# Row sums of a 64 MB array: the first load of SyncE in three transfers by partitions, and the first whole group on SyncE's queue

## Chip, core and metric

The kernel runs on one core of a Trainium2 chip. The metric is the device time of one execution in microseconds (us); lower is better. The core's engines follow their own instruction streams and meet at semaphores: VectorE (DVE in the profile), ScalarE (ACT), GpSimd (POOL), SyncE (SP) and TensorE (PE, without work here). Transfers between memory and the on-chip SBUF run on 16 DMA engines. SP, ACT and POOL each issue transfers on a queue of their own (q1, q10 and q0 in the profile), and all three queues use the same 16 engines. SBUF has 128 partitions.

## What is computed

The input x has 32 x 512 x 1024 float32 values. Each of the 16,384 rows of 1024 values is summed:

```python
def reference(x: np.ndarray) -> np.ndarray:
    return np.sum(x, axis=-1).astype(np.float32)
```

That is 67.11 MB read once, and 65 KB written.

## The kernel before

Each of the 128 partitions takes J = 128 rows. They lie in two regions: region a holds 16 rows of each partition (2,048 rows of x), region b the other 112. Within a region a partition's rows follow each other in memory, so that one partition's share of a transfer is one contiguous run. `rows_from(j, n)` names rows j to j + n of every partition.

There are three buffers `bufs` of 16 rows for each partition (64 KB). The work goes in this order:

- the entry load: 8 rows of each partition (FIRST = 8, the first half of the last group, `tail` = 112), 4.19 MB, into buffer 0, issued by SP at line 97 through `load(..., "first")`;
- groups 0 to 6, each 16 rows of each partition, 8.39 MB, into buffers 1, 2, 0, 1, 2, 0, 1, issued by POOL at line 99;
- the last 8 rows of each partition, as four transfers of lines 175 to 181, into buffer 2 and the tile `ends`, issued by POOL at line 99 too.

`issue_first_load_at_entry` (lines 9 to 27) works on the finished program. It takes the first DMA instruction of SP that it finds behind the entry block, and puts it into the entry block ahead of SP's drain, that is, ahead of the barrier at which all engines meet before the kernel's body begins. It moves one instruction and returns.

DVE takes the entry load and groups 0 to 5 in that order (lines 171 to 173): it waits for the load's semaphore, sums all rows with one `tensor_reduce` (line 106), and adds one to the semaphore `summed`. Group 6 and the last 8 rows form the tail. DVE sums rows of it with `halves` (line 115) and ACT with `act` (line 135), each row by itself, as the transfers land.

A group's load may start when its buffer is free. POOL issues groups 0 and 1 at once, since their buffers are empty, and waits for `summed` to reach g - 1 before group g from group 2 on (lines 152 and 153). Group 2 so waits for the entry load's sum, group 3 for that of group 0, and so on. The four last transfers wait for `summed` to reach 6 (line 174), the sum of group 4.

ACT stores the sums of groups 0 to 6 and of the entry load near the end, as two transfers (lines 210 and 211). The last store is SP's (line 227), and SP's wait for it is the last instruction.

Of the kernel before, what the change touches and what calls it, by code (L numbers as in the profile page):

```python
# [30 lines left out]
def kernel(  # L31
# [5 lines left out]
    nc = tc.nc  # L37
# [12 lines left out]
    BIG = 16  # L50
# [15 lines left out]
    def rows_from(j, n):  # L66
        if j < ONE:
            return x_a[:, j : j + n, :]
        return x_b[:, j - ONE : j - ONE + n, :]

    last = J // BIG - 1
    tail = last * BIG
    FIRST = 8
# [14 lines left out]
    def semaphore(name):  # L88
        return ctx.enter_context(nc.semaphore(name=name))

    def block_of(t, a, n):
        return t[:, a * dim : (a + n) * dim].rearrange("p (n d) -> p n d", d=dim)

    def load(dst, src, k):
        sem = semaphore(f"load_{k}")
        if k == "first":
            nc.sync.dma_start(out=dst, in_=src).then_inc(sem, 16)
        else:
            nc.gpsimd.dma_start(out=dst, in_=src, single_packet=True).then_inc(sem, 16)  # L99
        return sem  # L100

    summed = semaphore("summed")

    def vec(j, block):
        n = block.shape[1]
        return nc.vector.tensor_reduce(  # L106
            out=sums[:, j : j + n],
            in_=block,
            axis=mybir.AxisListType.X,
            op=mybir.AluOpType.add,  # L110
        )
# [31 lines left out]

    t = bufs[0]
    block = block_of(t, 0, FIRST)
    landed = load(block, rows_from(tail, FIRST), "first")
    loads = [(landed, tail, block)]
    for g in range(last):  # L150
        t = bufs[(1 + g) % 3]
        if g > 1:
            nc.gpsimd.wait_ge(summed, g - 1)
        block = block_of(t, 0, BIG)
        loads.append((load(block, rows_from(g * BIG, BIG), g), g * BIG, block))

# [3 lines left out]
    t = bufs[(1 + last) % 3]  # L162
# [5 lines left out]
    whole6, whole8 = ends[:, :six], ends[:, six:]  # L168
    right6, right8 = whole6[:, 1:-1], whole8[:, 1:-1]
    nc.vector.memset(ends[:, six - 1 :: whole8.shape[-1]], 0.0)  # L170
    for landed, first, block in loads[:-1]:
        nc.vector.wait_ge(landed, 16)
        vec(first, block).then_inc(summed, 1)
    nc.gpsimd.wait_ge(summed, last - 1)
    line = rows_from(j, 8).rearrange("p n d -> p (n d)")
# [1 line left out]
            (right6, 5 * dim + SIXTH), (right8, 7 * dim + EIGHTH))  # L177
    five, seventh, sixth, eighth = (
        load(dst, line[:, at : at + dst.shape[-1]], f"run_{k}")
        for k, (dst, at) in enumerate(runs)  # L180
    )
# [3 lines left out]

    paired = semaphore("paired")
    carried = semaphore("carried")
    landed, first, block = loads[-1]
    n_pairs = 10
    nc.vector.wait_ge(landed, 16)  # L190
    for q in range(n_pairs):
# [67 lines left out]
```

## Time and profile before

| what | us |
|---|---|
| median of 3 runs | 160.6 (160.52 to 160.64) |
| the profiled execution | 160.88 |
| span of the profiled execution | 159.6 |
| DVE busy | 121.6 (76% of the span) |
| ACT busy | 11.0 (7%) |
| POOL busy | 6.2 (4%) |
| DVE's idle time before sums of line 106, all ended by a load | 32.2, of which 22.9 before the first sum |
| POOL's idle time at line 99 ended by sums of DVE | 120.9 |
| issue to landing, SP's entry load | 24.5 |
| issue to landing, the seven groups, median | 40.5 |

Reading from HBM was 67.11 MB, on average 421 GB/s over the span. The span starts with SP's issue of the entry load. A DMA's issue is a short instruction on the engine that issues it; what the transfer takes is the time to its landing. A packet here is one partition's contiguous run: 32 KB in the entry load, 64 KB in a group. The records of the trace give each packet its start, duration, queue and size, but not its engine.

### The profile page before, as it was taken

How to read it: one execution, taken by the hardware profiler on the slowest of the kernel's cores; microseconds unless marked ns; L12 is line 12 of the kernel's file. 1: busy time of each engine (PE TensorE's matmuls, PEld its weight loads, DVE VectorE, ACT ScalarE, POOL GpSimd, SP SyncE). 2: the span in 40 equal slices, each digit the busy share in tenths (PEclk: the TensorE clock that was granted, in tenths of full speed). 3: DMA queues.
4: the chain of work that ended last, by engine and by line, in shares of the span. 5: the costliest groups of instructions: out<-in, count | busy, mean ns of one | idle time of the engine just before them, and what ended most of it. 6: DMA issues, size and time to landing. Idle time of an engine off the chain costs nothing.

```text
span 159.6 us, 123 instructions
## 1 busy us (share of the span) xinstructions
DVE 121.6 (76%) x42; ACT 11.0 (7%) x19; POOL 6.2 (4%) x15
## 2 busy tenths in 40 slices
DVE  0000008999998999949999499986999679995986
ACT  3000000000000000000000000000000000000995
POOL 3000000010001000010000100010000220000000
DMA  7999996996997979969969969969969979898993
GB/s 263 526 394 394 435 600 279 526 509 279 526 444 345 526 345 444 526 279 509 526 263 526 526 263 526 509 279 526 509 279 526 460 329 526 378 411 364 438 402 127
DMA packets 2000, 67.18 MB, mean 421 GB/s; under 512 B 624, under 2 KB 624, under 8 KB 848
## 3 DMA queue, kind: packets, MB, share of 16 engines
q0 software_dynamic: 1424, 62.92, 91.2%
q1 hardware_dynamic: 288, 4.20, 6.6%
q10 hardware_dynamic: 288, 0.06, 0.2%
HBM read 67.11 MB, written 0.07 MB: 421 GB/s over the span
## 4 chain that ended last, share of the span: by engine, by line
DMA 74%; DVE 22%; POOL 1%; issue 1%; POOLq 0%
DMA rows<-in_x_dram 56%; DVE sums L106 22%; DMA ends<-in_x_dram 19%; POOL rows L99 1%; DVE ends L115 0%; DVE sums L115 0%; POOLq L43 0%
## 5 line engine op out<-in xcount | busy, mean ns | idle before, releaser
L106 DVE TENSOR_REDUCE sums<-rows 128x16 f32<-128x16384 f32 (+1 forms) x7 | 111.9, 15999 | 32.2 <-DMA rows<-in_x_dram 32.2
L135 ACT ACTIVATE unread<-rows 128x1024 f32<-128x1024 f32 x9 | 9.1, 1013 | 145.5 <-DMA rows<-in_x_dram 145.5
L115 DVE CUSTOM_DVE_ANT_0 rows<-rows 128x512 f32<-128x512 f32 (+2 forms) x15 | 9.0, 659 | 2.6 <-DMA rows<-in_x_dram 2.6
L99 POOL DMA_DIRECT2D rows<-in_x_dram x9 | 4.9, 546 | 122.4 <-DVE sums L106 120.9
L135 ACT ACTIVATION_READ_ACCUMULATOR unread<-rows 128x1 f32 x9 | 1.7, 186 | 0.0
L135 ACT ACT_TABLE_LOAD x1 | 1.3, 1283 | 1.4 <-PEq L43 1.4
L170 DVE MEMSET ends<- 128x2 f32 x1 | 0.1, 60 | 1.5 <-PEq L43 1.5
L115 DVE DVE_READ_ACCUMULATOR2_ANT sums<- 128x1 f32 x15 | 1.2, 80 | 0.0
L99 POOL DMA_DIRECT2D ends<-in_x_dram x2 | 1.1, 543 | 0.0
L115 DVE CUSTOM_DVE_ANT_0 ends<-ends 128x271 f32<-128x271 f32 (+1 forms) x2 | 0.7, 364 | 0.1
L115 DVE DVE_READ_ACCUMULATOR2_ANT ends<- 128x1 f32 x2 | 0.2, 84 | 0.0
L243 POOL MEMSET const-float32-0.0<- 128x1 f32 x1 | 0.1, 99 | 0.2 <-issue 0.2
L243 POOL MEMSET const-bfloat16-1.0<- 128x1 bf16 x1 | 0.1, 103 | 0.0
L243 POOL MEMSET const-float32-1.0<- 128x1 f32 x1 | 0.1, 99 | 0.0
L243 POOL MEMSET const-uint8-127<- 128x1 uint8 x1 | 0.1, 99 | 0.0
## 6 DMA issues: line engine op xcount, KB each, us to landing
rows<-in_x_dram SPq DMA_DIRECT2D x1, 4096.0 KB, 24.5
rows<-in_x_dram POOLq DMA_DIRECT2D x1, 2802.0 KB, 27.9
rows<-in_x_dram POOLq DMA_DIRECT2D x1, 899.0 KB, 29.6
ends<-in_x_dram POOLq DMA_DIRECT2D x1, 270.0 KB, 29.7
ends<-in_x_dram POOLq DMA_DIRECT2D x1, 125.0 KB, 29.5
rows<-in_x_dram POOLq DMA_DIRECT2D x7, 40.5
out_dram<-sums ACTq DMA_DIRECT2D x1, 48.0 KB, 1.6
out_dram<-sums ACTq DMA_DIRECT2D x1, 8.0 KB, 1.5
```

The source lines that it names most:

```text
L99: nc.gpsimd.dma_start(out=dst, in_=src, single_packet=True).then_inc(sem, 16)
L106: return nc.vector.tensor_reduce(out=sums[:, j : j + n], in_=block, axis=mybir.AxisListType.X, op=mybir.AluOpType.add,)
L115: return nc.vector.tensor_tensor_reduce(out=src[:, :n], in0=src[:, :n], in1=src[:, n:], scale=1.0, scalar=0.0, op0=mybir.AluOpType.add, op ...
L135: nc.scalar.activation(out=unread[n_acts % len(unread)][:, :], in_=src, func=mybir.ActivationFunctionType.Copy, accum_out=sums[:, j : j + ...
L170: nc.vector.memset(ends[:, six - 1 :: whole8.shape[-1]], 0.0)
L243: nc = _bacc.Bacc("TRN2", target_bir_lowering=False, num_devices=1)
```

## The change

The entry load becomes three transfers of SP on one semaphore: partitions 0, 4, 8, ... (32 of them), then 2, 6, 10, ... (32), then the odd ones (64). DVE waits for 48 instead of 16 before the first sum. Group 0 is issued by SP too, behind them. POOL's first load is then group 1, and it waits for `summed` to reach 1; group 2 waits for 1 as before. `issue_first_load_at_entry` isn't changed.

```diff
     def load(dst, src, k):
         sem = semaphore(f"load_{k}")
-        if k == "first":
+        if k == 0:
             nc.sync.dma_start(out=dst, in_=src).then_inc(sem, 16)
         else:
             nc.gpsimd.dma_start(out=dst, in_=src, single_packet=True).then_inc(sem, 16)
...
     t = bufs[0]
-    block = block_of(t, 0, FIRST)
-    landed = load(block, rows_from(tail, FIRST), "first")
-    loads = [(landed, tail, block)]
+    entry = semaphore("entry")
+    block, src = block_of(t, 0, FIRST), rows_from(tail, FIRST)
+    parts = ((0, 4), (2, 4), (1, 2))
+    for at, step in parts:
+        nc.sync.dma_start(out=block[at::step], in_=src[at::step]).then_inc(entry, 16)
+    loads = [(entry, 16 * len(parts), tail, block)]
     for g in range(last):
         t = bufs[(1 + g) % 3]
-        if g > 1:
-            nc.gpsimd.wait_ge(summed, g - 1)
+        if g > 0:
+            nc.gpsimd.wait_ge(summed, max(1, g - 1))
         block = block_of(t, 0, BIG)
-        loads.append((load(block, rows_from(g * BIG, BIG), g), g * BIG, block))
+        loads.append((load(block, rows_from(g * BIG, BIG), g), 16, g * BIG, block))
...
-    for landed, first, block in loads[:-1]:
-        nc.vector.wait_ge(landed, 16)
+    for landed, count, first, block in loads[:-1]:
+        nc.vector.wait_ge(landed, count)
         vec(first, block).then_inc(summed, 1)
...
-    landed, first, block = loads[-1]
+    landed, _, first, block = loads[-1]
```

## The prediction

> **What bounds the kernel now.** I read the chain of waits first, then the DMA part of the page, then the timeline, then the trace's records of single DMA packets. The chain that ended last, by engine and by line:
>
> ```profile
> DMA 74%; DVE 22%; POOL 1%; issue 1%; POOLq 0%
> DMA rows<-in_x_dram 56%; DVE sums L106 22%; DMA ends<-in_x_dram 19%; POOL rows L99 1%; DVE ends L115 0%; DVE sums L115 0%; POOLq L43 0%
> ```
>
> Three quarters of it is DMA. The 22% of DVE are two sums that freed a buffer for a load; they look like a bound and are none, because the load that they released stood behind another one in the same queue. The DMA queues and the time from issue to landing say so (columns: queue, packets, MB, share of 16 engines; then the issues):
>
> ```profile
> q0 software_dynamic: 1424, 62.92, 91.2%
> q1 hardware_dynamic: 288, 4.20, 6.6%
> ...
> rows<-in_x_dram SPq DMA_DIRECT2D x1, 4096.0 KB, 24.5
> ...
> rows<-in_x_dram POOLq DMA_DIRECT2D x7, 40.5
> ```
>
> 91.2% + 6.6% is 98% of what 16 engines can do in the span. A group load takes 40.5 us from issue to landing, though its bytes need half of that, so one whole group is always queued ahead. The timeline gives the pace (start, duration, engine, line, what, idle before it):
>
> ```profile
> 0.00 0.38 SPq L97 DMA_DIRECT2D rows<-in_x_dram  x1
> ...
> 1.44 1.28 ACT L135 ACT_TABLE_LOAD   x1 [1.44 <-PEq L43]
> ...
> 1.94 1.20 POOL L99 DMA_DIRECT2D rows<-in_x_dram  x2 [1.50 <-POOLq L43]
> 24.48 25.81 DVE L106 TENSOR_REDUCE sums<-rows 128x8 f32<-128x8192 f32 x2 [22.91 <-DMA rows<-in_x_dram]
> 33.46 0.53 POOL L99 DMA_DIRECT2D rows<-in_x_dram  x1 [30.31 <-DVE sums L106]
> 50.59 0.53 POOL L99 DMA_DIRECT2D rows<-in_x_dram  x1 [16.60 <-DVE sums L106]
> 51.08 17.22 DVE L106 TENSOR_REDUCE sums<-rows 128x16 f32<-128x16384 f32 x1 [0.79 <-DMA rows<-in_x_dram]
> 68.60 0.53 POOL L99 DMA_DIRECT2D rows<-in_x_dram  x1 [17.48 <-DVE sums L106]
> 70.43 17.22 DVE L106 TENSOR_REDUCE sums<-rows 128x16 f32<-128x16384 f32 x1 [2.13 <-DMA rows<-in_x_dram]
> ```
>
> The sums start at 51.08 and 70.43, 19.35 us apart, and so on to the tail. A group is 128 x 64 KB = 8.389 MB, and 8.389 MB in 19.35 us is 433.5 GB/s. In the packet records each engine moves 64 KB in 2.42 us; 8 of those are 19.36 us, the whole period. The engines never pause between groups. All 67.11 MB at 433.5 GB/s take 154.8 us and the chain's last load lands at 157.42, so only about 2.6 us of the load stream is not streaming. That start, a lower rate, or a DVE that falls behind are the only ways to move the end.
>
> The start in the packet records: the SP load is issued at 0.00, the 16 engines start their first 32 KB packet between 1.02 and 1.54, and end it between 2.89 and 3.21, but for one that ends at 3.52 (later such packets take 1.21). That laggard stays: at each group's landing 15 engines report within about 0.33 us and the last one 0.32 us after them.
>
> **The change part by part.**
>
> *Entry load in three pieces.* In the built program only the quarter of 32 partitions is ahead of the barrier; the second quarter, the half of 64 and group 0 follow behind SP's branch. So the stream starts with an instruction of the same kind at the same place. Its cost with 32 rows is not in the trace. Every SP and ACT issue here has 128 rows: 0.38 and 0.35 us on SP, 0.37 and 0.46 on ACT. From the end of the issue to the first packet it is 0.64 for the load and 0.50 for the stores. The farthest row is POOL's first issue, 0.67 against its later 0.53. I bound the shift of the stream by 0.2 us earlier (half of SP's 0.38 saved) and 0.3 later (0.67 less 0.38), and take 0, the nearest row.
>
> SP's later issues are hidden by the first quarter. ACT begins its first instruction behind the barrier at 1.44, POOL at 1.94. SP at 1.9 at the latest, plus 1.02 to the first packet, makes 2.9, while a quarter is two 32 KB packets per engine, 1.02 + about 1.95 + 1.22 = 4.2. The half is ready one issue later (3.3 to 3.6), group 0 another. Cover of 1.3 us; if it were gone, each us of delay would be a us of time.
>
> Two more transfers make two more seams in each engine's stream. The seams between groups cost 19.35 - 19.36 = 0, with a bound of 0.02 each from rounding. I take 0.
>
> *The laggard.* If its 0.3 us came from the first burst, the other order of descriptors may remove it (-0.3), keep it (0), or make another (+0.3). The first addresses that are read are mostly the same, so I take 0.
>
> *Group 0 on SP, behind the entry load.* Its 8.389 MB now run after the entry load instead of beside it. The entry load lands at about 2.7 + 4.194 MB / 433.5 GB/s = 12.4 instead of 24.48. DVE sums it in 8.69, to 21.1. POOL then issues groups 1 and 2 (before: group 1 at 2.6, group 2 at 33.46; line 152's wait is now ahead of group 1, and all of POOL's later loads are queued behind it). Group 0 still has bytes to move, so the engines don't run dry; the records of before show one 32 KB packet of SP's queue alternating with one 64 KB packet of POOL's. If group 0 goes as 64 KB packets, the queues share evenly from about 22.5: group 0 has 4.0 MB left, 8.0 MB pass, and it lands at 22.5 + 18.5 = 41.0, against about 31 before. POOL coming later makes that earlier (first packet at 26.0: 37.4).
>
> So DVE begins group 0 at 41.0 instead of 33.17, and has six sums of 17.23 us to the pairs, which cannot start before group 6 lands at 147.84. 41.0 + 103.4 = 144.4: 3.4 us to spare, and by group 5 (41.0 + 86.2 = 127.2 against its landing at 128.49) DVE waits for DMA again. The buffers come free later, at 58.2, 75.4, 92.7, 109.9 and 127.1, each more than 10 us before the load ahead lands (70.4, 89.8, 109.1, 128.5, 147.8). From 128.49 on nothing differs.
>
> *Sum:* 0 (issue) + 0 (seams) + 0 (laggard) + 0 (order) = no change. The profiled run took 160.88 us, its span 159.6, and 1.3 lie around it; the median of the runs is 160.6, 0.3 below the profiled one. I forecast 160.6. Bounds of this case: -0.3 and +0.3, 160.3 to 160.9.
>
> **The rivals.**
>
> 1. *The engines get in each other's way in the three pieces: slower.* For it: the full rate (16 x 64 KB in 2.42 us) is only shown for transfers over all 128 partitions; nothing shows how 32 or 64 strided rows are dealt out. If two engines meet on one way into SBUF in each step, the 4.194 MB run at half rate: 9.7 us more, 170.3; if the pairs get out of step and meet half of the time, 4.8 more, 165.4. It decides as soon as the pieces lose more than 0.3 us, 3% of their 9.7. [...] Chance 0.25.
> 2. *The start is cleaner: faster.* A shorter transfer is issued sooner, or the laggard goes: its lead of 0.3 gone is 160.3, all engines ending like the earliest (2.89 for 3.52) 160.0. For it: the end is that laggard's, all the way. Against: the first packet's extra 0.7 us is there with any number of rows. Chance 0.22.
> 3. *The entry issue takes longer with this form.* +0.3 or a little more by POOL's dearer issue, 160.9 to 161.2; the barrier, which waits for SP, then moves too. Chance 0.10.
> 4. *Group 0 gets a third of the engines.* If SP's queue carries its rows as 32 KB packets, as it does now, group 0 lands at 22.5 + 12.0 MB / 433.5 GB/s = 50.2. DVE ends its six sums at 153.6 and the tail's 9.6 us of work at 163.2 instead of 158.10: 165.7. Against: POOL's queue carries 64 KB rows in one packet. Chance 0.05.
>
> **How the numbers follow.** The forecast has 0.38. Less than 0.2% (0.3 us) is about what a measurement here can't tell from no change. Faster is rival 2: 0.22; same the forecast: 0.38; slower rivals 1, 3 and 4: 0.40. The range starts at 160.0 (all engines like the earliest) and ends at 165.8 (rival 4, and rival 1 at half effect). It leaves out the stronger half of rival 1 and a little of rival 2, some 0.17. The forecast's own range is 160.3 to 160.9.
>
> **What would show it.** Right: an SP issue near 0.38, first packets near 1.0 and no pause at the seams; the first sum at about 12.4, the second at 37 to 41; 19.35 us between the sums from group 5 on. The landing of the entry load tests rival 1: 22 us for half rate. The laggard's 0.3 us at the landings tests rival 2, SP's first issue rival 3, and a start of the second sum near 50 rival 4. I am wrong if the pieces run below 433 GB/s, if SP's second issue comes after about 3 us, or if DVE is still summing group 5 when group 6 has landed.

## The result, and the profile after

The changed kernel takes 161.81 us (median; 161.29 to 162.09) against 160.6 before: a ratio of 1.0073, 95% interval [1.0053, 1.0092]. It is slower by 1.2 us, and its runs spread more. The profiled execution took 161.69 us, with a span of 160.4; it lies 0.1 below its median, and the profiled one of before 0.3 above, so the two profiles differ by 0.8 us and not by 1.2.

The timeline of the changed kernel up to the sum of group 5 (start, duration, engine, line, what, idle before it), with the lines that answer to those of before:

```profile
0.00 2.94 SPq L152 DMA_DIRECT2D rows<-in_x_dram  x3
...
1.84 1.28 ACT L135 ACT_TABLE_LOAD   x1 [1.84 <-PEq L43]
...
2.99 0.58 SPq L97 DMA_DIRECT2D rows<-in_x_dram  x1
13.23 8.69 DVE L106 TENSOR_REDUCE sums<-rows 128x8 f32<-128x8192 f32 x1 [11.25 <-DMA rows<-in_x_dram]
22.22 1.20 POOL L99 DMA_DIRECT2D rows<-in_x_dram  x2 [21.79 <-DVE sums L106]
39.81 68.60 DVE L106 TENSOR_REDUCE sums<-rows 128x16 f32<-128x16384 f32 x4 [17.90 <-DMA rows<-in_x_dram]
...
109.96 17.22 DVE L106 TENSOR_REDUCE sums<-rows 128x16 f32<-128x16384 f32 x1 [1.55 <-DMA rows<-in_x_dram]
...
129.31 17.22 DVE L106 TENSOR_REDUCE sums<-rows 128x16 f32<-128x16384 f32 x1 [2.12 <-DMA rows<-in_x_dram]
```

Three things are to be seen. ACT starts behind the barrier 0.40 us later (1.84 for 1.44): SP's first issue ends at 0.54 instead of 0.38, and the way from there to the barrier's end is longer by the rest, 0.24. The entry load is complete at 13.2 (before: 24.5), so only half as long after its issue as before, since nothing is interleaved with it any more. And from 109.96 on DVE waits for each load again. The sum of group 5, at 129.31, starts 0.82 later than before (128.49), and the span is 0.8 longer: the whole loss of this profile is there before the tail begins.

The chain of waits, by engine and by line:

```profile
DMA 64%; DVE 32%; issue 1%; SPq 1%; POOL 1%
DMA rows<-in_x_dram 45%; DVE sums L106 32%; DMA ends<-in_x_dram 19%; SPq L152 1%; POOL rows L99 1%; DVE ends L115 0%; DVE sums L115 0%
```

DVE's share rises from 22% to 32%. That is no new bound: the chain runs through a sum that released a load which then stood in a queue, as before (issued at 74.45 and landed 35.48 us later, while a group's bytes take 19.36). The new entry is SPq L152, the issue of the second and third piece. In order of time (start, duration, what):

```profile
1.83 0.47 SPq L152
2.30 0.05 issue
2.35 0.59 SPq L152
```

The trace's records of DMA packets show where the stream lost its time (start + duration, 32 KB each where nothing stands behind it). They don't name the engine; a row is put together by taking the packet that starts where another one ends. Two of the 16 engines of the changed kernel, and one of before:

```
after   1.33+1.78 3.11+1.23 | 4.34+1.21 5.55+1.68 | 7.23+1.35 8.58+1.21 9.79+1.21 10.99+1.21 | 12.21+2.42(64 KB)
after   1.59+1.89 3.48+1.23 | 4.71+2.10 6.80+1.21 | 8.02+1.21 9.23+1.21 10.44+1.21 11.64+1.21 | 12.86+2.42(64 KB)
before  1.02+2.06 3.08+1.21   4.29+1.22 5.51+1.21   6.72+2.42(64 KB) 9.14+1.21
```

The bars are the seams between the transfers. The first packets start 0.3 us later than before. Both packets of the first quarter take no longer than before (1.78 to 1.89 and 1.23 in these rows, 2.06 and 1.21 in that of before). Behind the first seam packets take up to 2.10 instead of 1.21, on one engine at once and on the other a packet later. By about 11 us it is over, and group 0's 64 KB take the usual 2.42.

### The profile page after: what moved, and what is told of

Its sections match the earlier page's. It is cut to its first block, busy times and chain, and to the rows that moved or that the text cites. A ratio compares the mean times of both kernels' runs of the same rounds, so it can differ in the third digit from the quotient of the medians.

```text
span 160.4 us, 125 instructions
## 1 busy us (share of the span) xinstructions
DVE 121.4 (76%) x42; ACT 11.0 (7%) x19; POOL 5.6 (4%) x14
## 4 chain that ended last, share of the span: by engine, by line
DMA 64%; DVE 32%; issue 1%; SPq 1%; POOL 1%
DMA rows<-in_x_dram 45%; DVE sums L106 32%; DMA ends<-in_x_dram 19%; SPq L152 1%; POOL rows L99 1%; DVE ends L115 0%; DVE sums L115 0%
## 5 line engine op out<-in xcount | busy, mean ns | idle before, releaser
L99 POOL DMA_DIRECT2D rows<-in_x_dram x8 | 4.4, 548 | 123.7 <-DVE sums L106 123.7
```

## The experiments

Each kernel was timed in rounds with the kernel before on the same chip, and its ratio is to that. "Lead" below is the time from the start of the next transfer's issue to the moment at which the median engine reaches the seam, by the packet records.

### Order or pieces

The entry load as one transfer, the rest as changed:

```diff
-    parts = ((0, 4), (2, 4), (1, 2))
+    parts = ((0, 1),)
```

> The entry load is one transfer over 128 partitions again; group 0 stays on SyncE and GpSimd's waits stay. In the changed kernel's packets the first 32 KB of the engines end 0.25 us later than before, and the second and third transfer lose another 0.6 us; from group 0 on nothing is lost. If the whole loss belongs to the three pieces (theory A), this kernel takes 160.6 +- 0.15, with SP's first issue at 0.38 and first packets at 1.02 again. If the order of the queues (group 0 behind the entry load, group 1 waiting) costs something of its own (theory B), it takes 161.0 or more.

160.63 us, ratio 0.9995 [0.9986, 1.0003]. Its first sum starts at 12.11:

```profile
0.00 0.36 SPq L152 DMA_DIRECT2D rows<-in_x_dram  x1
1.42 0.33 SPq L97 DMA_DIRECT2D rows<-in_x_dram  x1
12.11 8.69 DVE L106 TENSOR_REDUCE sums<-rows 128x8 f32<-128x8192 f32 x1 [10.55 <-DMA rows<-in_x_dram]
```

That is 1.12 before the changed kernel's 13.23, nearly all of the 1.2 us. The start of the first sum is thus a good single reading for what the entry costs, as long as nothing is interleaved with the entry load.

The reverse, three pieces with group 0 on POOL and POOL's waits as before:

```diff
-        if k == 0:
+        if k == "none":
...
-        if g > 0:
-            nc.gpsimd.wait_ge(summed, max(1, g - 1))
+        if g > 1:
+            nc.gpsimd.wait_ge(summed, g - 1)
```

> Three pieces as in the changed kernel, but group 0 on GpSimd and its waits as before. Theory A (pieces alone): 161.4 to 162.0, like the changed kernel. Theory B (order): 160.6 to 160.9.

161.84 us, 1.0071 [1.0055, 1.0086], like the changed kernel. The pieces cost all of it; SyncE's group 0 and GpSimd's added wait cost nothing.

### What about the pieces: their place or their shape

All three ahead of the barrier (the helper moves three instructions instead of one):

```diff
-        load = insts.pop(at)
+        early = [insts[k] for k in at[:3]]
...
-        main.instructions = entry[:k] + [load] + entry[k:]
+        main.instructions = entry[:k] + early + entry[k:]
```

> As the changed kernel, but all three pieces are issued ahead of the barrier, one after the other. Theory C (the second and third piece are issued too late behind the barrier, at 1.83 and 2.35, so that the engines start them without having read ahead): with issues at about 0.54 and 1.05 the loss of 0.6 us goes, and 161.1 or less remain, the later first packet alone. Theory D (the strided pieces disturb each other on the engines whenever they are issued): 161.5 to 162.1, and the packets between 4.3 and 9 us still take 1.3 to 2.1 us instead of 1.21.

161.0 us, 1.0022 [1.0013, 1.003].

```profile
0.00 1.81 SPq L150 DMA_DIRECT2D rows<-in_x_dram  x3
...
3.12 0.35 SPq L95 DMA_DIRECT2D rows<-in_x_dram  x1
...
12.40 8.69 DVE L104 TENSOR_REDUCE sums<-rows 128x8 f32<-128x8192 f32 x1 [9.14 <-DMA rows<-in_x_dram]
```

0.8 of the 1.2 us are gone, though the barrier moves to 3.1 and with it group 0's issue. In the packet records every packet behind the first takes 1.21 or 1.22. The first packets still start at 1.33. This is theory C's outcome as to the time of the issue; that the engines read ahead was not shown.

Three pieces that each span all 128 partitions, at the places of the change:

```diff
-    parts = ((0, 4), (2, 4), (1, 2))
+    parts = ((0, 2), (2, 2), (4, 4))
-    for at, step in parts:
-        nc.sync.dma_start(out=block[at::step], in_=src[at::step]).then_inc(entry, 16)
+    for at, n in parts:
+        nc.sync.dma_start(out=block[:, at : at + n], in_=src[:, at : at + n]).then_inc(entry, 16)
```

> Three pieces of the same sizes, issued at the same places, but each spans all 128 partitions: rows 0 to 1, 2 to 3 and 4 to 7 (8, 8 and 16 KB for each partition). Theory D (strided partitions are to blame): 160.5 to 160.8, SP's first issue 0.38. Theory C (late issue behind the barrier): the loss of about 0.6 us at the second transfer stays, 161.1 to 161.5; only the start is that of before.

162.02 us, 1.0079 [1.0067, 1.0092]: theory D, that the stride disturbs the engines, falls. Theory C has the loss, but not its size: 1.4 us without any stride, above the 161.5 that it allowed, while the start is that of before (issue 0.37, first packets at 1.00).

Two theories were then set against each other. Theory C2: what counts is the lead, and one of about 2 us is too short. Theory E: every seam behind the barrier between small transfers costs about 0.7 us, whatever the lead. The same three pieces by rows, all ahead of the barrier:

> Three pieces by rows (2, 2, 4), all ahead of the barrier, issued at about 0, 0.4 and 0.8. Theory C2: both losses gone, 160.5 to 160.8, with SP's first issue 0.37 and no slow packets. Theory E: 161.2 to 162.0.

160.67 us, 1.0001 [0.9992, 1.001]. Both losses are gone, with three transfers and two more seams than with one. A seam cost nothing here where the next transfer had been issued early enough (3.8 us ahead at the first one).

### The stride alone, and contiguous pieces

Even partitions at the entry, odd ones behind the barrier, `parts = ((0, 2), (1, 2))`:

> Two strided pieces, even partitions at the entry, odd ones behind the barrier. The seam is reached near 6.9, a lead of more than 4 us, so theory C2 sees no loss there and leaves the strided first issue alone (0.54 instead of 0.37, first packets 0.3 later): 160.9 to 161.1. If the strided pieces cost more than their issue: 161.3 or more.

161.06 us, 1.0033 [1.0022, 1.0043]. With a seam at 7.0 (lead 5.2) only the late start is left: 0.44 us.

Contiguous pieces:

```diff
-    parts = ((0, 4), (2, 4), (1, 2))
-    for at, step in parts:
-        nc.sync.dma_start(out=block[at::step], in_=src[at::step]).then_inc(entry, 16)
+    parts = ((0, 32), (32, 64), (64, 128))
+    for lo, hi in parts:
+        nc.sync.dma_start(out=block[lo:hi], in_=src[lo:hi]).then_inc(entry, 16)
```

> The changed kernel with contiguous pieces: partitions 0 to 31, 32 to 63, 64 to 127. [...] If the partitions of a piece don't matter, 161.8 as with the strided ones, with a first issue of about 0.54.

170.95 us, 1.0641 [1.0626, 1.0655]. The windows of its profile (stretch, its length, busy times, clock, DMA share, GB/s), once while the entry load runs and once behind it:

```profile
4.00:20.00 16.00, 0.00 (x0) 0.00 (x0) 0.00 (x0) 1.00 0.95 197
30.00:50.00 20.00, 2.10 (x2) 0.00 (x0) 1.20 (x2) 1.00 0.97 419
```

The engines are as busy as ever (0.95) and move half as much: 32 KB packets take 2.56 us instead of 1.21. That is the half rate that rival 1 reckoned with, and its price of 9.7 us comes near the 10.3 measured. Strided pieces did not lose it: 32 KB packets of the three at the entry took 1.21 or 1.22 us. The runs show these rates, not their cause; that engines meet on the way into SBUF was not shown.

SP's first issue took 0.39 us for the contiguous quarter, 0.54 for the strided one, and 0.54 too for the 64 even partitions above; for 128 it took 0.36 to 0.38. What lengthened it in these kernels was the stride, not the number of rows.

### How early is early enough

With two pieces of four rows, `parts = ((0, 4), (4, 4))` by rows, the engines reach the seam at about 6.7:

> Two pieces over all 128 partitions, four rows each; the second is issued behind the barrier at about 1.42. The engines reach it near 6.5 instead of 4.0. Theory C2 (what counts is the lead: how long the next transfer has been issued when an engine comes to the seam; about 2 us is too short, 3 us enough): 160.5 to 160.8, no packet longer than its like. Theory E (every seam behind the barrier between small transfers costs about 0.7 us): 161.2 or more.

160.69 us, 1.0001 [0.9992, 1.001]. With one row and seven, it is reached at 3.0:

> One row at the entry, seven behind the barrier at about 1.42. The engines come to the seam near 2.9, a lead of about 1.1 us. Theory C2: a larger loss than with two rows, 162.0 or more, though it has one seam less. Theory E: one seam less than in the by-rows kernel of 162.0, so 161.3 or less.

162.46 us, 1.0121 [1.0102, 1.014]. One seam less than by twos and fours, and a larger loss: what counts isn't the number of seams.

Then the four-row kernel was held, with its seam at 6.7 each time, and SP's second issue moved by work of DVE in a free buffer, which is added to the kernel. `widths` is empty (late_0; SP then waits for 1, the clearing alone), 512 (late_half), 1024 (late_1), 1024 and 512 (late_1_half), or 1024 twice (late_2):

```diff
+    idle, held = bufs[2][:, :dim], semaphore("held")
+    nc.vector.memset(idle, 0.0).then_inc(held, 1)
+    nc.vector.wait_ge(held, 1)
+    for q, wide in enumerate(widths):
+        op = nc.vector.tensor_reduce(out=sums[:, q : q + 1], in_=idle[:, :wide],
+                                     axis=mybir.AxisListType.X, op=mybir.AluOpType.add)
+    op.then_inc(held, 1)
     for at, n in parts:
+        if at:
+            nc.sync.wait_ge(held, 2)
```

> Four and four rows, the second issued behind one clearing of 1024 columns, at about 2.7; the lead is about 3.5 us. Theory C2 (threshold between 2.3 and 3.2 us): 160.6 to 160.8. If any delay of this kind loses: 161.0 or more.

> The same behind a clearing and a sum of 512 columns, issue at about 3.4, lead about 2.8 us, between the threshold's bounds. Theory C2: 160.6 to 161.5, more than with the issue at 2.7 and less than the 161.9 with the issue at 3.91.

> Four and four rows as in the kernel that took 160.7, but SyncE holds the second transfer back until VectorE has cleared 1024 columns and summed them once, which adds work in a free buffer: the issue moves from 1.42 to about 3.0 to 3.8, and the engines still come to the seam near 6.5. Theory C2 (the lead alone counts): the lead shrinks from 4.7 to 2.4 to 3.1 us, at the edge: 160.6 to 161.5. Theory G (the size of the first piece counts, not the lead): 160.7.

> Issue at about 4.5, lead about 1.7 us. If the loss grew evenly with lateness: 162.0 or more. If it is largest where the engines still have some but not enough left (issue near 3.9) and falls behind that: 161.2 to 161.8.

> The same with two sums, the issue at 4.1 to 4.9 and a lead of 1.3 to 2.1 us. Theory C2: a loss like that of the kernels with such leads, 161.5 to 162.5. Theory G: 160.7.

| second issue at | engines reach the seam at | lead | us | ratio to before |
|---|---|---|---|---|
| 1.42 (four rows) | 6.64 | 5.2 | 160.69 | 1.0001 [0.9992, 1.001] |
| 2.66 (late_0) | 6.71 | 4.1 | 160.69 | 1.0005 [0.9996, 1.0015] |
| 3.37 (late_half) | 6.66 | 3.3 | 160.7 | 1.0002 [0.9993, 1.0011] |
| 3.91 (late_1) | 6.69 | 2.8 | 161.88 | 1.0078 [1.0066, 1.0091] |
| 4.50 (late_1_half) | 6.66 | 2.2 | 161.18 | 1.0036 [1.002, 1.0051] |
| 5.03 (late_2) | 6.59 | 1.6 | 161.05 | 1.0025 [1.0016, 1.0034] |
| 3.90 (late_1, group 0 held back) | 6.76 | 2.9 | 162.17 | 1.0094 [1.0079, 1.0109] |
| 1.83 (changed kernel) | 4.60 | 2.8 | 161.81 | 1.0073 [1.0053, 1.0092] |
| 1.42 (by rows, 2, 2, 4) | 4.18 | 2.8 | 162.02 | 1.0079 [1.0067, 1.0092] |
| 1.42 (one row and seven) | 2.97 | 1.6 | 162.46 | 1.0121 [1.0102, 1.014] |
| 0.60 (all at the entry) | 4.57 | 4.0 | 161.0 | 1.0022 [1.0013, 1.003], its late start |
| 0.42 (by rows, all at the entry) | 4.23 | 3.8 | 160.67 | 1.0001 [0.9992, 1.001] |
| 1.83 (even, then odd partitions) | 7.03 | 5.2 | 161.06 | 1.0033 [1.0022, 1.0043], its late start |

In one kernel, with the same bytes, moving the issue by 0.54 us (3.37 to 3.91) turns no loss into 1.2 us. DVE's added work isn't the cause: late_half has it too and loses nothing. The contiguous pieces aside, all kernels of this study sort by that: a lead of 3.3 or more loses nothing at the seam, one of 2.9 or less loses. (The row with group 0 held back is explained at the end of this section.) Theory C2 holds in this, and theories E and G fall.

How much is lost was not foreseen. At 3.37 no loss shows at all. The loss at 3.91 was above what theory C2 allowed (161.88 against 161.5), that at 5.03 below it (161.05 against 161.5), and the expectation that it grows with lateness missed: in this kernel it is largest just below the threshold and smaller behind it. The lead doesn't fix the size either, since a lead of 1.6 us costs 0.4 us here and 1.8 with one row and seven.

The issues of SP and the first sum on both sides of the threshold, for the issue at 3.37 and for the one at 3.91 (the second issue is the last 0.33 us of SP's line):

```profile
0.00 3.69 SPq L161 DMA_DIRECT2D rows<-in_x_dram  x2
...
12.17 8.69 DVE L106 TENSOR_REDUCE sums<-rows 128x8 f32<-128x8192 f32 x1 [8.82 <-DMA rows<-in_x_dram]
```

```profile
0.00 4.23 SPq L160 DMA_DIRECT2D rows<-in_x_dram  x2
...
13.40 8.69 DVE L106 TENSOR_REDUCE sums<-rows 128x8 f32<-128x8192 f32 x1 [9.51 <-DMA rows<-in_x_dram]
```

The DMA windows of the same two. A packet is counted where it begins, so a share can come out a little above 1:

```profile
7.00:10.00 3.00, 0.00 (x0) 0.00 (x0) 0.00 (x0) 1.00 1.02 437
```

```profile
7.00:10.00 3.00, 0.00 (x0) 0.00 (x0) 0.00 (x0) 1.00 0.93 344
```

In the packet records of the kernel with the issue at 3.91, five of the 16 engines stall at the seam: their next packet ends between 8.4 and 8.7, 1.2 to 1.5 us late. The other eleven pass the seam without a gap and are slowed later, between 8.4 and 10. With the issue at 5.03 all 16 pass, with 0.04 to 0.5 us lost on each. In both kernels the loss is near that of the slowest engines (1.2 us for up to 1.5, 0.4 for up to 0.5), so a few that stalled cost more here than all of them a little late.

Whether group 0's issue, 0.38 us behind the second one, makes the loss at 3.91 was tried by holding group 0 back to 6.15, behind three sums:

> The second transfer is issued at 3.9 as in the kernel that took 161.9, but group 0 follows only at about 6.3 instead of 4.28. If group 0's issue right behind the second transfer makes the loss: 160.7 to 161.1. If the moment of the second transfer alone makes it: 161.7 to 162.1.

162.17 us, 1.0094 [1.0079, 1.0109], with the lead at 2.9. Group 0 isn't the cause: the loss is 1.5 us, and the time lies just above the 162.1 that was expected if the moment of the second transfer alone makes it. In its packets, too, only a few engines stall (two by 0.9 and 1.5 to 1.7 us), and the others are hardly slowed. The later slowing of the other eleven engines was gone with group 0's early issue, and the time was not shorter for it. Why only some engines stall at a lead of 2.8 us, and why a shorter lead costs less in this kernel, stays open.

None of these kernels beats the kernel before; five match it.

## Why the prediction was wrong

The forecast was no change, 160.6, with bounds of 160.3 and 160.9. The kernel took 161.81: inside the wide range that the rivals gave, but slower, and outside those bounds.

- *What bounds the kernel:* right. Against the kernel with one entry load, the first sum is 1.12 us later and the span 1.1 longer, so the loss at the entry went through to the end and nothing behind it mattered.
- *Order, group 0 on SP, GpSimd's waits:* right, and in size. The first whole group was forecast to land between 37.4 and 41.0 and did at 39.8; DVE has caught up by group 4. The undoing of this part changed nothing (161.84 against 161.81).
- *Seams at 0:* right for seams with a transfer that has long been issued (160.67 with three pieces at the entry). The rows it was read from, the seams between groups, are of that kind, since a whole group is always queued ahead there.
- *"SP's later issues are hidden by the first quarter", with "cover of 1.3 us":* this is the step that failed. It took the time from the issue to the first packet at an idle start (1.02) as what the next transfer needs, and put the quarter's end at 4.2. The quarter ended even later, at 4.6, and the second piece was issued at 1.83, earlier than the 1.9 assumed. But with the engines running a lead of 2.8 us was not enough in these kernels; 3.3 was. In place of 1.3 us of cover up to 0.5 were missing, and that cost 0.8 us (161.81 against 161.0). The sign that the text gave for this, a second issue after about 3 us, was set by the same mistake.
- *The entry issue at 0, "the nearest row":* wrong in size. With the strided quarter SP's issue took 0.54 instead of 0.38, the first packets came at 1.33 instead of 1.02, and kernels that have this alone are slower by 0.38 and 0.44. The upper bound of 0.3 held the shift of the packets and fell a little short of that of the time; rival 3 had the mechanism. The cause isn't the smaller number of rows, which the text treated as the unknown, but the stride.
- *The laggard:* it was read as a lasting trait of the kernel. The kernel with one entry load and the same median shows 0.09 us of it in its own profile, and the profiled run of before lay 0.28 above its median; it was most likely a trait of that one execution, though no second profile of before shows it.
- *Rival 1* was no part of this. That strided pieces run at the full rate was the author's estimate, as the profile before has only transfers over 128 partitions; with all three at the entry, every packet behind the first took 1.21 or 1.22 us, as before. Contiguous pieces show rival 1's loss (2.56 us for a packet, 10.3 in all), though not the cause that it gave.

0.4 (start) + 0.8 (seam) = 1.2 us, the measured difference. The seam's part was taken away alone (161.0 left) and both parts together (160.67). The 0.8 is the price in this kernel and not a fixed one: pieces by rows, with the start of before and a lead of 2.8 too, lost 1.4 at the seam.

## What to carry to other kernels

In a kernel whose DMA stream never pauses, a cut in the first transfer bought nothing here and opened a place where the stream lost time (0.4 to 1.8 us) unless the following transfer had been issued well before the engines came to the cut. On SP's queue here 3.3 us was enough and 2.9 was not; the 1.0 us that the first packet of an idle queue took does not tell it. What lost nothing here was a cut by rows over all partitions with the pieces issued together (160.67 us). Slices of partitions cost the rate here if they were contiguous (half of it) and a later start if they were strided (0.4 us).

## What the runs showed that was not expected

- The needed lead has a sharp edge: between 3.3 and 2.8 us the same kernel goes from no loss to 1.2 us, and at 1.6 us its loss is back to 0.4.
- Just below the edge single engines stall for 0.9 to 1.7 us while most pass the seam without a gap.
- SP's first issue took 0.54 us for 32 strided partitions, 0.39 for 32 contiguous ones, and 0.36 to 0.38 for 128.
- Strided pieces, issued together, ran at full rate behind their first packets (1.21 or 1.22 us for 32 KB); contiguous ones at half of it (2.56 us, 205 GB/s between 16 and 20 us).
